# Embedding norm applied on turned rows, with three projection blocks pulled ahead

## The chip, the cores and the metric

The kernel runs on one core of one Trainium2 chip. The metric is device time of one execution in microseconds (us). The core has five engines that each run their own instruction list in order: PE (matrix products and transposes), DVE, ACT and POOL (element-wise work) and SP, which here only issues transfers. Transfers (DMAs) run beside them on queues.

## The reference

The program is two blocks in a row on 1024 tokens of 1024 channels. The first block, cut to what matters:

```python
x = layer_norm(x, ln_emb_g, ln_emb_b)            # (x - mean) * rsqrt(var + eps) * g + b
z = x @ w_in                                     # 1024 x 1984
xs, gs, cq, ckv, kr, gm = split(z)               # 512, 512, 256, 128, 64, 512 channels
ys = s5_branch(xs, ...) * silu(gs)               # state-space model, 32 groups of 16 channels
ym = mla_branch(cq, ckv, kr, ...) * silu(gm)     # latent attention, 4 heads
u  = ALPHA * x + concat(ys, ym) @ w_out
x  = layer_norm(u + sigmoid(u @ w_pg) * (p @ w_pp), ln_g, ln_b)
```

So the normalised x is needed twice: turned (channels on partitions) for `w_in`, and as rows much later, in `u`. The second block (dilated attention, a gated recurrence, a mixture of experts) is not touched.

## The kernel before

**Products.** Everything is fp32, and PE multiplies a shorter type (fp32r). Each operand is therefore split in a high and a low part, and each product is three matmuls: high·high (L178), low·high (L179), high·low (L180). A split takes an ACT copy (the high part, L146 or L150) and a DVE subtraction (the low part, L147 or L153).

**Weights.** `Chunks` loads a weight in chunks of 256 columns (SP, `wraw`, L167), two buffers, and splits each on ACT (`wh`) and DVE (`wl`). `ch.next()` hands out a chunk and issues the loads and splits of the one after it.

**First stage** (`block1`). The eight row tiles x0 to x7 (128 tokens each) are loaded, and the norm's weight and offset are loaded as `lng` and `lnb`, broadcast over 128 partitions (512 KB each). By pairs of tiles, `ln_stats` takes mean and reciprocal deviation on DVE (L443 to L450, and a Newton root, L192 to L205); ACT standardises (L313), POOL multiplies by `lng` (L314), DVE adds `lnb` (L315). The result goes to DRAM as `d_xln` for the much later `u`, and `transpose8` turns it on PE (L215) and splits it into `xTh`, `xTl`.

**Projection and s5.** The `w_in` projection is 32 blocks of 24 matmuls of 128x512 into PSUM (`psG`), 768 in all. The first eight (the `xs` channels, `g_xs`) go through DRAM (`d_xu`) to the s5 branch. `weave` merges three streams by declared costs: `s5_prep` and `s5_groups`; the projection; and rotary tables with small norms. `s5_prep` is a long chain of DVE work on tables (exponentials, sines, `er`, `ei`, `KB`, `KS`), of which line L266 is the first after the exponential's prologue. `s5_groups` runs eight groups; each builds `X1p` (L948), turns it on PE (L965), multiplies (L973, L993), has DVE and its scan make Z and A (L995 to L1004), and multiplies again (L1009 to L1011). The projection's matmuls stand between L993 and L1009 of a group and so fill PE there.

The framework puts each engine's instructions in a fixed order before the run; on the chip an engine waits at the head of its list.

**out_ple** (from L673). The s5 output comes back as `ysf` tiles and is split; the eight row tiles `u` (512 KB each) are loaded from `d_xln`. For each of four blocks of 256 columns and each of eight row tiles, PE makes a block of 24 matmuls of 128x256, and DVE adds it onto `u` (L705). `psG` has few buffers, so PE can go on only as DVE takes the finished blocks.

Of the kernel before, what the change touches and what calls it, by code (L numbers as in the profile page):

```python
# [271 lines left out]
def block1(c):  # L272

    tc, nc, I = c.tc, c.nc, c.I
    d = c.dram
    d_xln = c.d_xln = d.tile([S, D], FT, name="d_xln")
    d_c = c.d_c = d.tile([512, S], FT, name="d_c")
    d_gs = c.d_gs = d.tile([512, S], FT, name="d_gs")
    d_gm = c.d_gm = d.tile([512, S], FT, name="d_gm")
# [11 lines left out]
    xTh = [xp.tile([128, 4, S], FR, name=f"xTh{q}") for q in range(2)]  # L291
    xTl = [xp.tile([128, 4, S], FR, name=f"xTl{q}") for q in range(2)]
    xT = lambda k, sl: (xTh[k // 4][:, k % 4, sl], xTl[k // 4][:, k % 4, sl])
    W = I["w_in"]
    ch = Chunks(c, [(s, 8, True) for s in (
        [W[:, 0:256]], [W[:, 256:512]], [W[:, 1024:1280]], [W[:, 1280:1408], W[:, 1408:1472], W[:, 1408:1472]],
        [W[:, 512:768]], [W[:, 768:1024]], [W[:, 1472:1728]], [W[:, 1728:1984]])]
        + [([I["w_glu"][:, h:h + 256]], 4, False) for h in (0, 256)])

    with ExitStack() as es:  # L300
        pp = c.pool(es, "p0")
        X = [pp.tile([128, D], FT, name=f"x{m}") for m in range(NT)]
        for m in range(NT):
            nc.sync.dma_start(X[m], I["x"][m * 128:(m + 1) * 128, :])
        g_b = pp.tile([128, D], FT, name="lng")
        b_b = pp.tile([128, D], FT, name="lnb")
        nc.scalar.dma_start(g_b, bcast_rows(I["ln_emb_g"], D))
        nc.scalar.dma_start(b_b, bcast_rows(I["ln_emb_b"], D))
        for m0 in range(0, NT, 2):
            for m, (_, mb, r) in zip((m0, m0 + 1), ln_stats(c, X[m0:m0 + 2])):  # L310
                ms = slice(m * 128, (m + 1) * 128)
                x = X[m]
                nc.scalar.activation(x, x, AF.Identity, bias=mb, scale=r)  # L313
                nc.gpsimd.tensor_tensor(x, x, g_b, op=OP.mult)  # L314
                nc.vector.tensor_add(x, x, b_b)  # L315
                nc.sync.dma_start(d_xln[ms, :], x)
                c.dbg("xln", x, lambda o: o[ms, :])
                c.transpose8(x, True, lambda q: (xTh[q][:, :, ms], xTl[q][:, :, ms]))
            if m0 == 2:
                ch.ahead(1)  # L320


    d_xu = c.d_xu = d.tile([8, 128, 4, 128], FT, name="d_xu")
    stage = c.pool(es1, "st", 2)
    half = [slice(0, 512), slice(512, 1024)]
    cols = lambda wk, mb: (wk[0][:, mb * 128:(mb + 1) * 128], wk[1][:, mb * 128:(mb + 1) * 128])
# [4 lines left out]
        nc.scalar.activation(th[:, :n], ps, AF.Tanh, scale=0.5)  # L331
        nc.vector.scalar_tensor_tensor(dst, th[:, :n], 1.0, ps, op0=OP.add, op1=OP.mult)

    def g_xs(n):
        w = ch.next()
        for mb in range(2):
            o = stage.tile([128, 8, 128], FT, name="xo")
            for i, h in enumerate(half):
                ps = c.ps()
                c.gemm(ps, [(cols(w[k], mb), xT(k, h)) for k in range(8)])  # L340
                c.evac(o[:, :, 64 * i:64 * i + 64], ps.rearrange("p (n t) -> p t n", t=8))
                yield 5.2
            for g in range(8):
                b, gg = divmod(16 * n + 8 * mb + g, 4)
                nc.scalar.dma_start(d_xu[b, :, gg, :].rearrange("(t c) n -> c t n", t=8), o[16 * g:16 * g + 16])


    lv = c.con.tile([128, 3, NT], FT, name="lv")
# [7 lines left out]
    def g_latents(js):  # L356
        w = ch.next()
        late = None
        for i, h in enumerate(half):
            for mb, j in enumerate(js):  # L360
                ps = c.ps()
                c.gemm(ps, [(cols(w[k], mb), xT(k, h)) for k in range(8)])
                o = stage.tile([128, 512], FT, name="co")
                nc.vector.tensor_copy(o, ps)
                if late:
                    squares(*late)
                    late = None
# [42 lines left out]
    def rest(cost):  # L410
        yield cost

    gate = lambda o, ps: silu2(o, ps, 512)

    weave((seq(s5_prep(c, es1), s5_groups(c, es1)), 160.0),
          (seq(g_xs(0), g_xs(1), g_latents((0, 1)), g_latents((2, 3)),
               g_feat(d_gs, 0, gate), g_feat(d_gs, 256, gate), g_feat(d_gm, 0, gate), g_feat(d_gm, 256, gate)), 166.4),
          (seq(rest(120.0), rotary_tables(), latent_norms()), 180.0))
    wg = ch.next(), ch.next()
    es1.close()  # L420
# [2 lines left out]
    yp = c.pool(esy, "ym")  # L423
# [6 lines left out]
def seq(*gens):  # L430
    for g in gens:
        yield from g


def ln_stats(c, X):

    nc = c.nc
    n = len(X)
    mv = c.sm([128, n, 2], name="bmv")
    for i, x in enumerate(X):  # L440
        st = c.sm([128, 2, 6], name="bst")
# [231 lines left out]
def out_ple(c, ym, esy):  # L673
    tc, nc, I = c.tc, c.nc, c.I
# [3 lines left out]
    es = ExitStack()  # L678
# [5 lines left out]
    u = [up.tile([128, D], FT, name=f"u{m}") for m in range(NT)]  # L684
    uT = []
    yp = c.pool(esy, "ys")
    ys = [(yp.tile([128, S], FR, name=f"ysh{j}"), yp.tile([128, S], FR, name=f"ysl{j}")) for j in range(4)]
    ns = [slice(n * 256, n * 256 + 256) for n in range(4)]
    ch = Chunks(c, [([I["w_out"][:, s]], 8, False) for s in ns] + [([I["w_pg"][:, s]], 8, True) for s in ns])
    ch.ahead(1)  # L690
    for j in range(4):
        for hs in (slice(0, 512), slice(512, 1024)):
            f = yp.tile([128, 512], FT, name="ysf", bufs=3)
            nc.sync.dma_start(f, c.d_ys[j * 128:(j + 1) * 128, hs])
            c.split(ys[j][0][:, hs], ys[j][1][:, hs], f, scale=0.25)
    for m in range(NT):
# [1 line left out]
    mix = lambda k, m: tuple(a[:, m * 128:m * 128 + 128] for a in (ys + ym)[k])  # L698
    order = (4, 5, 6, 7, 0, 1, 2, 3)
    for n in range(4):  # L700
        w = ch.next()
        for m in range(NT):
            ps = c.ps((128, 256))
            c.gemm(ps, [(mix(k, m), w[k]) for k in order])
            nc.vector.scalar_tensor_tensor(u[m][:, ns[n]], u[m][:, ns[n]], ALPHA, ps, op0=OP.mult, op1=OP.add)  # L705
            if n == 3:
                if m % 2 == 0:
                    uT.append(alloc_aT())
                js = slice((m % 2) * 128, (m % 2) * 128 + 128)
# [50 lines left out]
    g_b = q.tile([128, D], FT, name="plg")  # L760
    b_b = q.tile([128, D], FT, name="plb")
# [4 lines left out]
    w = ch.next(), ch.next()  # L766
    for m in range(NT):
# [4 lines left out]
        x = u[m]  # L772
        ms = slice(m * 128, (m + 1) * 128)
# [25 lines left out]
def s5_prep(c, es):  # L799

    nc, I = c.nc, c.I
# [12 lines left out]
    with ExitStack() as es2:  # L814
        p = c.pool(es2, "s5p")
# [7 lines left out]
        ps = c.psum_tile("T", [128, 2, GR])  # L823
# [47 lines left out]
        nc.vector.tensor_scalar(t["sei"], t["ei"], sg, None, op0=OP.mult)  # L871
        yield 10.0

        q = [p.tile([128, GR], FT, name=f"q{i}") for i in range(5)]
        nc.vector.tensor_mul(q[0], ar, ar)
        nc.vector.tensor_mul(q[1], ai, ai)
        nc.vector.tensor_add(q[0], q[0], q[1])
# [159 lines left out]
class Chunks:  # L1037
# [9 lines left out]
    def next(self):  # L1047
        self.n += 1
        self.ahead(self.n + 1)
        w, self.w[self.n - 1] = self.w[self.n - 1], None  # L1050
        return w
# [957 lines left out]
```

## Time and profile before

| | |
|---|---|
| three runs | 2082.92, 2084.36, 2086.16 us; median 2084.36 |
| the profiled execution | 2080.49 us, of which 2078.7 lie between first and last instruction |
| PE, DVE, ACT, POOL busy | 92%, 72%, 49%, 15% of the span |
| mean granted TensorE clock | 0.958 |
| stages by PE's list | first stage and front of the projection to 195.6, s5 groups to 312.3, `out_ple` from about 495 |

How to read it: PE's share is a mean. Almost all of PE's idle time that bears on the change lies in the first 70 us, where PE waits for the norm, and in short waits up to 520 us. An idle stretch of another engine costs nothing unless PE waits for it later.

### The profile page before, as it was taken

To read this page: it belongs to the slowest core of one execution; us is meant where nothing else is said; L and a number is where in the kernel's file an instruction comes from. 1 tells how busy PE (TensorE), PEld (TensorE's weight loads), DVE (VectorE), ACT (ScalarE), POOL (GpSimd) and SP (SyncE) were. 2 spreads that over 40 slices of the span, in tenths; PEclk is the share of its full clock that TensorE was granted. 3 is DMA by queue.
4 is the path that set the end of the run, shared out by engine and by line. 5 is a ranking of instruction groups with operands and counts; after the bars stand their busy time and mean duration, and the time that the engine had idled before them with its cause. 6 is when DMAs were issued, how large, how long until landed. Compare 5 with 4: busy or idle time off the path is not lost.

```text
span 2078.7 us, 34559 instructions
## 1 busy us (share of the span) xinstructions
PE 1922.5 (92%) x13242; PEld 1705.7 (82%) x13242; DVE 1487.3 (72%) x2909; ACT 1023.7 (49%) x1572; POOL 316.5 (15%) x241
## 2 busy tenths in 40 slices
PE   2999998999999979999999999997899999999992
PEld 2777886888999978898999888897788888888881
DVE  7387677775244967656564556578999999999995
ACT  3223334453132334534432223145788888888883
POOL 3013520000000000000010000013322222222211
PEclk9899999999999989999999998899899999999996
DMA  4344536113131121111111113177899999999974
GB/s 175 100 121 135 157 104 203 41 42 125 44 112 41 59 90 48 57 56 50 48 37 32 42 37 105 61 257 254 302 374 375 379 372 374 358 366 370 355 291 171
DMA packets 143510, 349.14 MB, mean 168 GB/s; under 512 B 33792, under 2 KB 87680, under 8 KB 118768
## 3 DMA queue, kind: packets, MB, share of 16 engines
q1 hardware_dynamic: 127296, 323.81, 43.4%
q0 software_dynamic: 11152, 19.97, 4.0%
q10 hardware_dynamic: 4896, 3.15, 0.7%
q8 instruction: 105, 1.72, 0.3%
q14 instruction: 61, 0.50, 0.1%
HBM read 304.24 MB, written 54.01 MB: 172 GB/s over the span
## 4 chain that ended last, share of the span: by engine, by line
PE 48%; issue 25%; DVE 14%; POOL 5%; DMA 3%; ACT 3%; SPq 0%; POOLq 0%; DVEq 0%; ACTq 0%
PE psG L178 11%; PE psG L179 10%; PE psG L180 10%; POOL gates L1865 3%; PE psT L1303 2%; PE psPO L1254 2%; PE psPO L1387 2%; POOL xg L1865 1%; PE psPO L638 1%; DVE wl L147 1%; PE psSC L1233 1%; DMA wraw<-w_in 1%; PE psSC L1234 1%; PE psT L215 1%; DVE bst L443 1%
## 5 line engine op out<-in xcount | busy, mean ns | idle before, releaser
L1900 DVE TENSOR_TENSOR el<-raw,eh 128x1024 fp32r<-128x1024 f32 x384 | 446.1, 1219 | 31.6 <-ACT eh L1899 31.0
L1899 ACT ACTIVATE eh<-raw 128x1024 fp32r<-128x1024 f32 x384 | 396.8, 1060 | 62.1 <-PE psY L180 25.4
L178 PE MATMUL psG<-aTh,wh 128*128 128x256 f32 x640 | 187.1, 292 | 0.0
L179 PE MATMUL psG<-aTl,wh 128*128 128x256 f32 x640 | 183.6, 287 | 0.0
L180 PE MATMUL psG<-aTh,wl 128*128 128x256 f32 x640 | 183.6, 287 | 0.0
L146 ACT ACTIVATE wh<-wraw 128x512 fp32r<-128x512 f32 (+1 forms) x148 | 91.2, 624 | 181.3 <-PE psG L180 79.1
L147 DVE TENSOR_TENSOR wl<-wraw,wh 128x512 fp32r<-128x512 f32 (+1 forms) x148 | 104.9, 716 | 65.4 <-ACT wh L146 53.5
L178 PE MATMUL psG<-wh,aTh 128*128 128x256 f32 x512 | 146.0, 285 | 0.0
L179 PE MATMUL psG<-wl,aTh 128*128 128x256 f32 x512 | 144.7, 283 | 0.0
L180 PE MATMUL psG<-wh,aTl 128*128 128x256 f32 x512 | 144.1, 281 | 0.0
L178 PEld LDWEIGHTS psG<-aTh,wh 128*128 128x128 f32 x640 | 124.4, 194 | 4.8 <-issue 3.9
L180 PEld LDWEIGHTS psG<-aTh,wl 128*128 128x128 f32 x640 | 124.2, 194 | 1.9 <-issue 1.4
L179 PEld LDWEIGHTS psG<-aTl,wh 128*128 128x128 f32 x640 | 124.4, 194 | 1.4 <-issue 0.9
L180 PE MATMUL psG<-xTh,wl 128*128 128x512 f32 x256 | 103.9, 406 | 4.4 <-DVE wl L147 4.4
L178 PE MATMUL psG<-xTh,wh 128*128 128x512 f32 x256 | 103.7, 406 | 2.1 <-ACT wh L146 1.8
L178 PE MATMUL psY<-eh,hh 128*128 128x512 f32 x256 | 103.0, 402 | 1.7 <-ACT hh L150 1.7
L179 PE MATMUL psG<-xTl,wh 128*128 128x512 f32 x256 | 103.3, 403 | 0.1
L178 PE MATMUL psUU<-eh,xh 128*128 128x512 f32 x256 | 102.8, 402 | 0.0
L178 PE MATMUL psGG<-eh,xh 128*128 128x512 f32 x256 | 101.2, 395 | 0.7 <-ACT xh L146 0.7
L180 PE MATMUL psGG<-eh,xl 128*128 128x512 f32 x256 | 100.9, 394 | 0.0
L180 PE MATMUL psY<-eh,hl 128*128 128x512 f32 x256 | 100.6, 393 | 0.0
L179 PE MATMUL psGG<-el,xh 128*128 128x512 f32 x256 | 100.5, 393 | 0.0
(538 smaller groups left out, 5282.2 us busy)
## 6 DMA issues: line engine op xcount, KB each, us to landing
raw<-w_gate SPq DMA_DIRECT2D x64, 1024.0 KB, 21.6
raw<-w_down SPq DMA_DIRECT2D x64, 1024.0 KB, 22.3
raw<-w_up SPq DMA_DIRECT2D x63, 1024.0 KB, 21.4
wraw<-w_in SPq DMA_DIRECT2D x52, 256.0 KB, 3.0
wraw<-w_in SPq DMA_DIRECT2D x68, 128.0 KB, 2.5
wraw<-w_out SPq DMA_DIRECT2D x32, 256.0 KB, 2.6
x<-x SPq DMA_DIRECT2D x8, 512.0 KB, 8.1
d_xln<-x SPq DMA_DIRECT2D x8, 512.0 KB, 2.6
```

The costliest lines, as they stand in the source:

```text
L146: nc.scalar.activation(h, src, AF.Copy)
L147: nc.vector.tensor_sub(l, src, f32(h))
L178: mm(ps, ah, bh, start=first, stop=False)
L179: mm(ps, ah, bl, start=False, stop=False)
L180: mm(ps, al, bh, start=False, stop=last)
L215: self.nc.tensor.transpose(ps[:, i, :], src, self.ident)
L1254: nc.tensor.matmul(po[64 * j:64 * j + 64], v[:, k, (b % 2) * 128 + 64 * j:(b % 2) * 128 + 64 * j + 64], et[j][:, i, :], start=k == 0, stop ...
L1303: nc.tensor.transpose(ps[:, i, :], e[:, (k0 + i) * 128:(k0 + i + 1) * 128], c.ident)
L1387: nc.tensor.matmul(po[a, cc * 32:cc * 32 + 32], st[a], qi[a, cc * 32:cc * 32 + 32], start=False, stop=cc == cs[-1], skip_group_check=True)
L1865: c.nc.gpsimd.indirect_dma_start(out=dst, out_offset=None, in_=src, in_offset=bass.IndirectOffsetOnAxis(ap=idx, axis=0), bounds_check=src. ...
L1899: nc.scalar.activation(h, src, AF.Copy)
L1900: nc.vector.tensor_sub(l, src, f32(h))
```

## The change

The norm's weight and offset are no longer applied to rows. `standard` only standardises, and `d_xln` holds these plain rows. `turn(h)` turns 512 tokens at a time: per block j of 128 channels four transposes fill one PSUM bank, ACT makes the high part g·x+b as it evicts (L359), and DVE makes the low part in two steps, g·x minus the high part (L361) and plus b (L362). There the weights stand along partitions, so g and b are one number per partition; `lngb` holds them, loaded as 2 x 1024 single elements on ACT's queue. `g_xs` now takes two weight chunks at once and yields by blocks: channel blocks 0 to 2 of the first 512 tokens are issued ahead of the second `turn`. Block 2's halves go out as separate transfers (40 `d_xu` transfers instead of 32). `out_ple` applies weight and offset to `u`: two broadcast loads of 128 KB (`eg`, `eb`) and 16 DVE operations of 128x256 per column block. `ysf` has two buffers instead of three, and s5's table `q` three tiles of its own and two borrowed ones.

```diff
-        g_b = pp.tile([128, D], FT, name="lng")
-        b_b = pp.tile([128, D], FT, name="lnb")
-        nc.scalar.dma_start(g_b, bcast_rows(I["ln_emb_g"], D))
-        nc.scalar.dma_start(b_b, bcast_rows(I["ln_emb_b"], D))
-        for m0 in range(0, NT, 2):
-            for m, (_, mb, r) in zip((m0, m0 + 1), ln_stats(c, X[m0:m0 + 2])):
-                ms = slice(m * 128, (m + 1) * 128)
-                x = X[m]
-                nc.scalar.activation(x, x, AF.Identity, bias=mb, scale=r)
-                nc.gpsimd.tensor_tensor(x, x, g_b, op=OP.mult)
-                nc.vector.tensor_add(x, x, b_b)
-                nc.sync.dma_start(d_xln[ms, :], x)
-                c.transpose8(x, True, lambda q: (xTh[q][:, :, ms], xTl[q][:, :, ms]))
-            if m0 == 2:
-                ch.ahead(1)
+        gb = pp.tile([128, 2, 8], FT, name="lngb")
+        nc.scalar.dma_start(gb[:, 0], I["ln_emb_g"].rearrange("(j p) -> p j", p=128))
+        nc.scalar.dma_start(gb[:, 1], I["ln_emb_b"].rearrange("(j p) -> p j", p=128))
+        def standard(ms):
+            for m, (_, mb, r) in zip(ms, ln_stats(c, [X[m] for m in ms])):
+                nc.scalar.activation(X[m], X[m], AF.Identity, bias=mb, scale=r)
+                nc.sync.dma_start(d_xln[m * 128:(m + 1) * 128, :], X[m])
+        def turn(h):
+            hs = slice(h * 512, h * 512 + 512)
+            for j in range(8):
+                ps = c.psum_tile("T", [128, 512])
+                for m in range(4):
+                    nc.tensor.transpose(ps[:, m * 128:m * 128 + 128], X[4 * h + m][:, j * 128:j * 128 + 128], c.ident)
+                th, tl = xT(j, hs)
+                g, b = gb[:, 0, j:j + 1], gb[:, 1, j:j + 1]
+                nc.scalar.activation(th, ps, AF.Identity, bias=b, scale=g)
+                lo = pp.tile([128, 512], FT, name="lo", bufs=3)
+                nc.vector.scalar_tensor_tensor(lo, ps, g, f32(th), op0=OP.mult, op1=OP.subtract)
+                nc.vector.tensor_scalar(tl, lo, b, None, op0=OP.add)
+        standard((0, 1))
+        standard((2, 3))
+        ch.ahead(1)
+        turn(0)
+        standard((4, 5, 6, 7))
+        xs = g_xs()
+        for _ in range(3):
+            next(xs)
+        turn(1)
...
+    def g_xs():
+        w = ch.next(), ch.next()
+        o = {}
+        for q, i in ((0, 0), (1, 0), (2, 0), (0, 1), (1, 1), (2, 1), (3, 0), (3, 1)):
+            ps = c.ps()
+            c.gemm(ps, [(cols(w[q // 2][k], q % 2), xT(k, half[i])) for k in range(8)])
...
     weave((seq(s5_prep(c, es1), s5_groups(c, es1)), 160.0),
-          (seq(g_xs(0), g_xs(1), g_latents((0, 1)), g_latents((2, 3)),
-               g_feat(d_gs, 0, gate), g_feat(d_gs, 256, gate), g_feat(d_gm, 0, gate), g_feat(d_gm, 256, gate)), 166.4),
+          (seq(xs, g_latents((0, 1)), g_latents((2, 3)),
+               g_feat(d_gs, 0, gate), g_feat(d_gs, 256, gate), g_feat(d_gm, 0, gate), g_feat(d_gm, 256, gate)), 150.8),
...
-            f = yp.tile([128, 512], FT, name="ysf", bufs=3)
+            f = yp.tile([128, 512], FT, name="ysf", bufs=2)
...
     for n in range(4):
+        g_n, b_n = (yp.tile([128, 256], FT, name=f"e{q}") for q in "gb")
+        nc.sync.dma_start(g_n, bcast_rows(I["ln_emb_g"][ns[n]], 256))
+        nc.sync.dma_start(b_n, bcast_rows(I["ln_emb_b"][ns[n]], 256))
         w = ch.next()
         for m in range(NT):
             ps = c.ps((128, 256))
             c.gemm(ps, [(mix(k, m), w[k]) for k in order])
+            nc.vector.tensor_tensor(u[m][:, ns[n]], u[m][:, ns[n]], g_n, op=OP.mult)
+            nc.vector.tensor_tensor(u[m][:, ns[n]], u[m][:, ns[n]], b_n, op=OP.add)
             nc.vector.scalar_tensor_tensor(u[m][:, ns[n]], u[m][:, ns[n]], ALPHA, ps, op0=OP.mult, op1=OP.add)
```

DVE's list at the start of s5's long chain (L266), before: six projection blocks have been copied out by then, the last two of them as `xo`.

```order
L261 TENSOR_SCALAR exr<-exr 128x32
L141 COPY xo<-psG 128x8x64 x2
L147 TENSOR_TENSOR wl<-wraw,wh 128x512 x2
L266 TENSOR_SCALAR exk<-exr 128x32
L267 RECIPROCAL exk<-exk 128x32
L268 SCALAR_TENSOR_TENSOR exr<-exr,exk 128x32
```

The same place after (L391 is the copy of a latent block's `psG`):

```order
L261 TENSOR_SCALAR exr<-exr 128x32
L147 TENSOR_TENSOR wl<-wraw,wh 128x512 x2
L141 COPY co<-psG 128x512
L141 COPY xo<-psG 128x8x64
L391 COPY co<-psG 128x512 x3
L266 TENSOR_SCALAR exk<-exr 128x32
L267 RECIPROCAL exk<-exk 128x32
```

L266 moved behind the copies of eleven blocks (264 matmuls) from behind six (144). On PE the first group's transposes (L965, now L998) moved from behind 480 projection matmuls to behind 534.

PE's list at the last group of s5, after (L998, L1006, L1026 and L1042 to L1044 are the former L965, L973, L993 and L1009 to L1011):

```order
L1042 MATMUL psT<-Mt_1487,U 128x128
L1043 MATMUL psT<-Q_2356,A_1489 128x128
L1044 MATMUL psT<-Q_2357,A_1490 128x128
L998 MATMUL psT<-ident,X1p 128x128 x4
L1006 MATMUL psT<-Q_2515,KB 16x128 x4
L1026 MATMUL psT<-U,BT_2533 128x128 x4
L1026 MATMUL psT<-U,BT_2534 128x128 x4
L1042 MATMUL psT<-Mt_1488,U 128x128
```

Before, 29 projection matmuls stood between the L993 and the L1009 of this group, and 36 in the group ahead of it; now there are none and 12. The earlier groups have 36 to 39.

SP's list at the start of `out_ple`, before (u_4605 is the first row tile of eight):

```order
L694 DMA ysf<-d_ys 128x512 x3
L697 DMA u_4605<-d_xln 128x1024
L694 DMA ysf<-d_ys 128x512 x3
L697 DMA u_4606<-d_xln 128x1024
L694 DMA ysf<-d_ys 128x512 x2
L697 DMA u_4607<-d_xln 128x1024
```

Here `u` follows three `ysf` loads at a time, and nothing stands behind the last `u`. The end of the same piece after:

```order
L724 DMA u_4606<-d_xln 128x1024
L724 DMA u_4607<-d_xln 128x1024
L721 DMA ysf<-d_ys 128x512 x2
L724 DMA u_4608<-d_xln 128x1024
L724 DMA u_4609<-d_xln 128x1024
L730 DMA eg<-ln_emb_g 128x256
L731 DMA eb<-ln_emb_b 128x256
```

The row tiles are now u_4602 to u_4609. The `ysf` loads go by twos with two `u` loads behind each pair, and the first `eg` and `eb` stand behind all of them.

## Rows read from the trace of the kernel before

**Rows 1.** Stretches by time: busy us (instructions) of each engine, PE's granted clock, DMA share, GB/s

```profile
0.00:63.00 63.00, 21.25 (x88) 16.52 (x88) 51.12 (x108) 22.20 (x30) 21.38 (x12) 0.92 0.45 173
50.00:60.00 10.00, 8.22 (x34) 6.56 (x34) 9.70 (x10) 5.34 (x9) 4.91 (x2) 0.67 0.57 210
103.50:195.60 92.10, 84.58 (x376) 69.95 (x374) 77.73 (x190) 28.85 (x46) 19.16 (x19) 0.93 0.42 125
195.60:312.30 116.70, 116.34 (x705) 100.54 (x706) 79.17 (x140) 38.79 (x77) 45.60 (x34) 0.98 0.48 133
510.00:520.00 10.00, 7.52 (x60) 7.31 (x61) 3.37 (x8) 1.26 (x2) 0.00 (x0) 1.00 0.93 334
```

**Rows 2.** Groups by line and shape, 0 to 70 us: busy us, mean ns, idle before

```profile
L314 POOL TENSOR_TENSOR x<-x,lng 128x1024 f32<-128x1024 f32 x8 | 21.2, 2665 | 35.0 <-ACT x L313 35.0
L315 DVE TENSOR_TENSOR x<-x,lnb 128x1024 f32<-128x1024 f32 x8 | 16.9, 2145 | 2.3 <-POOL x L314 2.3
L215 PE MATMUL psT<-ident,x 128*128 128x128 f32 x64 | 13.2, 378 | 38.1 <-DVE x L315 35.0 <-DVE xTl L147 3.1
```

**Rows 3.** Timeline of DVE, first stage: start, duration, instruction, idle before

```profile
19.33 2.33 DVE L205 SCALAR_TENSOR_TENSOR rs_o<-rs_b,rs_o 128x2 f32<-128x2 f32 x1
...
21.66 2.31 DVE L195 TENSOR_SCALAR rs_h<-bve 128x2 f32<-128x2 f32 x1
...
25.57 0.14 DVE L450 SCALAR_TENSOR_TENSOR bmb<-bmv,brs 128x2 f32<-128x2 f32 x1
...
60.43 1.22 DVE L315 TENSOR_TENSOR x<-x,lnb 128x1024 f32<-128x1024 f32 x1
```

**Rows 4.** Timeline of PE, to 200 us

```profile
27.38 1.97 PE L215 MATMUL psT<-ident,x 128*128 128x128 f32 x8 [27.38 <-DVE x L315]
...
53.75 0.63 PE L179 MATMUL psG<-xTl,wh 128*128 128x512 f32 x1
54.17 0.63 PE L180 MATMUL psG<-xTh,wl 128*128 128x512 f32 x1
...
63.16 0.99 PE L178 MATMUL psG<-xTh,wh 128*128 128x512 f32 x2 [0.24 <-ACT xTh L146]
...
165.16 0.39 PE L180 MATMUL psG<-xTh,wl 128*128 128x512 f32 x1
165.38 0.39 PE L178 MATMUL psG<-xTh,wh 128*128 128x512 f32 x1
...
195.63 1.09 PE L965 MATMUL psT<-ident,X1p 128*128 128x128 f32 x4 [4.65 <-DVE X1p L948]
```

**Rows 5.** Timeline of DVE, 98 to 215 us

```profile
101.64 0.69 DVE L141 COPY xo<-psG 128x512 f32<-128x512 f32 x1 [12.91 <-PE psG L180]
103.45 0.17 DVE L266 TENSOR_SCALAR exk<-exr 128x32 f32<-128x32 f32 x1
...
123.24 0.43 DVE L232 TENSOR_SCALAR sdk<-sdk 128x512 f32<-128x512 f32 x1
```

**Rows 6.** What DVE waited for, 103.4 to 195.5 us: us in total, times, longest

```profile
DVE co L364 <- PE psG L180: 4.8, 2, 2.7
DVE xo L141 <- PE psG L180: 2.4, 1, 2.4
```

**Rows 7.** Timeline of DVE in the last s5 group

```profile
302.78 0.67 DVE L995 TENSOR_TENSOR Z<-psT,cos 128x512 f32<-128x512 f32 x1
...
308.11 0.74 DVE L1004 SCALAR_TENSOR_TENSOR A<-Z,cst,sin 128x508 f32<-128x508 f32 x1
```

**Rows 8.** Timeline of DVE at the start of `out_ple`

```profile
518.11 0.42 DVE L705 SCALAR_TENSOR_TENSOR u<-u,psG 128x256 f32<-128x256 f32 x1 [0.87 <-DMA u<-d_xln]
```

**Rows 9.** Timeline of PE at the start of `out_ple`

```profile
514.18 0.39 PE L178 MATMUL psG<-wh,ymh 128*128 128x256 f32 x1 [0.94 <-DVE u L705]
```

**Rows 10.** DMA issues by line: count, KB each, median us from issue to landing

```profile
ysf<-d_ys SPq DMA_DIRECT2D x8, 256.0 KB, 3.4
gq<-q_norm_g SPq DMA_DIRECT2D x1, 1.0 KB, 8.9
lb<-hgrn_gamma SPq DMA_DIRECT2D x1, 4.0 KB, 3.0
```

More of the change, by code (lines that the diff above doesn't have):

```diff
@@ L294, in block1 @@
     W = I["w_in"]
-    ch = Chunks(c, [(s, 8, True) for s in (
+    ch = Chunks(c, [(s, 8, False) for s in (
         [W[:, 0:256]], [W[:, 256:512]], [W[:, 1024:1280]], [W[:, 1280:1408], W[:, 1408:1472], W[:, 1408:1472]],
@@ L298, in block1 @@
         + [([I["w_glu"][:, h:h + 256]], 4, False) for h in (0, 256)])
[L300 to L304, printed above, removed]
-        g_b = pp.tile([128, D], FT, name="lng")
-        b_b = pp.tile([128, D], FT, name="lnb")
-        nc.scalar.dma_start(g_b, bcast_rows(I["ln_emb_g"], D))
-        nc.scalar.dma_start(b_b, bcast_rows(I["ln_emb_b"], D))
-        for m0 in range(0, NT, 2):
-            for m, (_, mb, r) in zip((m0, m0 + 1), ln_stats(c, X[m0:m0 + 2])):
-                ms = slice(m * 128, (m + 1) * 128)
-                x = X[m]
-                nc.scalar.activation(x, x, AF.Identity, bias=mb, scale=r)
-                nc.gpsimd.tensor_tensor(x, x, g_b, op=OP.mult)
-                nc.vector.tensor_add(x, x, b_b)
-                nc.sync.dma_start(d_xln[ms, :], x)
-                c.dbg("xln", x, lambda o: o[ms, :])
-                c.transpose8(x, True, lambda q: (xTh[q][:, :, ms], xTl[q][:, :, ms]))
-            if m0 == 2:
-                ch.ahead(1)
     d_xu = c.d_xu = d.tile([8, 128, 4, 128], FT, name="d_xu")
@@ L332, in silu2 @@
         nc.vector.scalar_tensor_tensor(dst, th[:, :n], 1.0, ps, op0=OP.add, op1=OP.mult)
[L334 to L345, printed above, removed]
+    def g_xs():
[4 more added lines that the diff above has]
+            c.gemm(ps, [(cols(w[q // 2][k], q % 2), xT(k, half[i])) for k in range(8)])
+            n0, n1 = 64 * i, 64 * i + 64
+            if q == 2:
+                d = stage.tile([128, 512], FT, name="co").rearrange("p (t n) -> p t n", t=8)
+                full, first, last = d, n0, True
+            else:
+                if i == 0:
+                    o[q] = stage.tile([128, 8, 128], FT, name="xo")
+                full, first, last = o[q], 0, i == 1
+                d = full[:, :, n0:n1]
+            c.evac(d, ps.rearrange("p (n t) -> p t n", t=8))
+            yield 5.2
+            for g in range(8 if last else 0):
+                b, gg = divmod(8 * q + g, 4)
+                nc.scalar.dma_start(d_xu[b, :, gg, first:n1].rearrange("(t c) n -> c t n", t=8), full[16 * g:16 * g + 16])
@@ new lines, in block1 @@
+    with ExitStack() as es:
+        pp = c.pool(es, "p0")
+        X = [pp.tile([128, D], FT, name=f"x{m}") for m in range(NT)]
+        for m in range(NT):
+            nc.sync.dma_start(X[m], I["x"][m * 128:(m + 1) * 128, :])
+        gb = pp.tile([128, 2, 8], FT, name="lngb")
[26 more added lines that the diff above has]
+        turn(1)
@@ L872, in s5_prep @@
         yield 10.0
-        q = [p.tile([128, GR], FT, name=f"q{i}") for i in range(5)]
+        q = [p.tile([128, GR], FT, name=f"q{i}") for i in range(3)] + [dt, dr]
         nc.vector.tensor_mul(q[0], ar, ar)
```

## The prediction

> **What bounds the kernel now.** I read the stretches by time first [rows 1]. In the first 63 us PE is busy 21.3; from 195.6 to 312.3 it is busy 116.3 of 116.7. So the first stage is bound by what feeds PE, and the s5 groups by PE. The groups by line name the feeder: PE's transposes wait 35.0 us for DVE's `lnb` addition (L315), which waits for POOL's multiplication at 2.67 us each [rows 2]. PE's timeline gives two marks: transposes begin at 27.38, and steady matmuls at 63.16, when 26 of the 768 projection matmuls are done [rows 4]. Between 103.5 and 195.6 PE is busy 84.6 of 92.1 and DVE 77.7 [rows 1]; there the question is which comes last. PE then waits 4.65 us at 195.63 for `X1p` [rows 4], so DVE's s5 chain ends last; but DVE itself stood 7.2 us for PE's blocks [rows 6], so the two held each other up. At the start of `out_ple` transfers take 0.93 of the queues and PE is busy 7.5 of 10 [rows 1].
>
> **First stage.** Eight POOL operations (21.2 us) and eight DVE additions (16.9) go [rows 2]. They also held other work. Two operations on 128x2 take 2.33 and 2.31 us at 19.33 and 21.66, while POOL multiplies from 19.3; a like one takes 0.14 at 25.57 [rows 3]. The L315 addition takes 1.22 once POOL has ended [rows 3], 2.15 in the mean [rows 2]. The Trainium skill (SBUF — State Buffer, "SBUF: two separate sides") says that GpSimd and VectorE share a port pair under an exclusive lock and the loser blocks. These rows agree; with POOL out of this stage the inflation should vanish altogether.
>
> So the statistics of x2, x3, ready at 25.6, come at 25.6 − 4.3 ≈ 21.3, and two normalisations put x3 at about 24. PE can begin turning then instead of alternating with L315. DVE now needs per channel block L361 (128x512) and L362. A 128x512 `TENSOR_SCALAR` took 0.43 [rows 5]; the old subtraction starts every 0.60. No row has L362's rounded output. Below, the plain 0.43, started every 0.34; above, 0.60 like the subtraction. I take the first, since it is the nearest instruction. Then one `turn` is 8 × 0.94 = 7.5 us of DVE (9.6 above), plus weight splits in between, and ends near 35 (37 to 39). Three blocks of 24 matmuls at 0.227 [rows 4] are 16.3 us; they follow the tiles closely and end near 46. The second `turn` ends near 54, with 105 matmuls issued. Against 26 at 63.16 PE is 9 us early and 79 × 0.227 = 18 us of work further: a lead of 27 us.
>
> **What becomes of the lead.** This decides the forecast. s5's chain cannot start early, because L266 now stands on DVE behind eleven blocks (264 matmuls) rather than six (144). Before, 144 were done at 101.6 [rows 5]: from 63.16, 118 matmuls took 38.5 us, of which 118 × 0.227 = 26.8 and the other 11.7 small transposes and slow-clock matmuls. After: 159 × 0.227 = 36, plus about 10, from 54 makes 100. L266 gains only about 3 us on its 103.45 [rows 5].
>
> From L266 to `X1p` took 92.1 us, 77.7 of it DVE's own work [rows 1]. The 7.2 us of waits for PE [rows 6] go, as PE is ahead, and about 1 us of block copies lies ahead of L266 now. The waits for POOL and ACT stay. So 92.1 − 8.2 ≈ 84, and `X1p` is ready at 184 instead of 195.5. PE has to give back most of its lead waiting for weight splits (`wl`) that stand among the same DVE operations. Bounds: 7 us less if the chain follows at DVE's pure busy time (177), 6 more if waits for PE stay (190). Gain at the first group: 11 us (5 to 18).
>
> At that point 534 projection matmuls stand ahead in PE's order, not 480: 54 × 0.227 = 12.3 us less is left. But they were cover. In the last group 6.1 us passed on DVE between the first Z and the end of A [rows 7], with a copy and a weight split of 0.6 each in it; alone some 4.6. The last group now has no matmuls to hide that, the one ahead 12 × 0.227 = 2.7 us: 4.6 + 1.9 ≈ 6 us of waiting returns (4 to 9). Front gain: 11 + 12.3 − 6 ≈ 17 us (10 to 25).
>
> Two edits I cost at nothing: s5's shared `q` tiles, and eight more `d_xu` issues on ACT, which is busy 28.9 of 92 us [rows 1]. Without that cover, and each as long as a 128x512 subtraction (0.6 from start to start), they would be 5 us.
>
> **out_ple.** Sixty-four DVE operations of 128x256 are added, each near the 0.42 of the existing one [rows 8]: 27 us, beside PE's matmuls, DVE being a third busy [rows 1]. Hidden, except at the start. The first block's `u` needs `eg` and `eb`, and these stand last in SP's list, behind all eight `u` loads. Before, the second `psG` round began at 514.18, one `u` tile being enough [rows 9], and the fifth landed at about 518 [rows 8], with the queues at 0.93 and 334 GB/s [rows 1]. Two `ysf` buffers also make SP issue by pairs: load (3.4 us [rows 10]), split, next pair, three times over. So `eg` lands about 520 (517.5 to 521), and three operations later, near 522, PE has a free `psG`: 8 us lost (4 to 11). Nothing else on PE's list can fill it. Later columns' pairs have 23 us each, and cost nothing. This time counts as if nothing were shifted; the front gain moves all of it alike.
>
> **Sum.** From the profiled 2080.5: −11 − 12.3 + 6 + 8 ≈ −9.3, or 2071.2. That execution was 3.9 below the median, so about 2075 in the median runs.
>
> **Rivals.**
> A. PE keeps its lead. If DVE's chain is not what ends last, the whole 27 us pass on, less 8 in `out_ple`: 2065. For it: DVE is idle 14 us between 103 and 195. Against: PE already waits for `X1p`, and the chain's start moves by 3 only. A hidden `eg` wait (transfers landing with the `u` tiles) leads to 2067 in the same way. Together 0.18.
> B. Gain too small to tell: `X1p` at 190 and both losses at their upper ends, −5.6 − 12.3 + 9 + 11 ≈ +2, to −3: 2081 to 2088. Chance 0.18.
> C. Slower, by PE's clock. The first stage's matmuls now alternate with transposes and waits for two evicting engines. In the 50 to 60 stretch, with just such alternation, the granted clock was 0.67 [rows 1] and matmuls stood 0.43 apart instead of 0.227 [rows 4], which is PE at the lower of its two levels. If all 105 run so, 105 × 0.2 = 21 us are lost before the second `turn` ends, and L266, behind the 264th matmul, starts at 121, not 100. Then `X1p` comes at 205: 2075 + 21 ≈ 2096. In general the gain is 110 minus L266's start, so it turns at 110, and beyond 114 is seen as slower. For it: that row. Against: PE has 16 us of matmuls in one stretch without waits. Chance 0.09.
> D. `lngb` lands late. Its loads are of single elements. An element-wise load of 1024 elements (`lb`) took 3.0 us, one of 256 (`gq`) 8.9 [rows 10]; by the latter's pace 36 us. ACT needs it at 24; landing at 38, it would cost 14 us, at 2089. The Trainium skill (DMA: Bandwidth & Descriptors, "Rules for kernel authors") warns that a non-contiguous last dimension becomes one descriptor per element. The row for `lb` bears out the form but not a high price. Chance 0.05.
>
> **How the numbers follow.** Forecast (2068 to 2081) 0.50, A 0.18, B 0.18, C 0.09, D 0.05. A change under 0.2% (4.2 us) can't be told from none here: faster is below 2080.2, slower above 2088.5. Faster takes A and most of the forecast, 0.65; slower C, half of D and a part of B, 0.14; the same 0.21. The range 2062 to 2088 leaves out C's centre and the ends; the forecast's own is 2068 to 2081.
>
> **What would show it.** Right: the first L356 transposes near 19 to 25; the second `turn` over by 57; L266 near 100; a wait of 10 us of PE for `wl` near 110; first L998 near 185; waits of 2 and 4.6 us ahead of L1042 in the last two groups; 8 us of PE waiting for `u` in `out_ple`. Wrong: L266 after 110, small operations on DVE still taking over 2 us, `eg` landing before the last `u` tile, or no wait for `wl` (then A).

## The result and the profile after

The changed kernel took 2097.87 us, the median of 5 runs (2094.76 to 2102.8), against 2084.36 for the kernel before: a ratio of 1.0067 [1.0054, 1.0079], so 13.5 us slower where 2075 was forecast. The profiled execution's span is 2095.9 us (2078.7 before), 17.2 more; the profiled execution of the kernel before lay 3.9 below its median, so 13.5 is the measure of the whole, and the two traces serve to say where it arises. Three marks on DVE, read in both traces, say where: the last attention copy `yo` starts 5.0 us later than before (505.04 against 500.07), `out_ple`'s first `u` with the projection 14.6 later (528.28, L738, against 513.72), and the first `wpr` load 17.15 later (620.27 against 603.12). After that nothing moves. So the front, where −17 was forecast, gave +5, and `out_ple`, where +8 was forecast, gave about +12.

Stretches of the changed kernel (from:to, length, then busy us and instructions of PE, weight load, DVE, ACT, POOL; PE's granted clock, DMA share, GB/s). The first two are those of [rows 1]; the last runs from the first turned `X1p` to the end of s5:

```profile
0.00:63.00 63.00, 44.16 (x205) 35.03 (x206) 43.88 (x128) 29.70 (x39) 0.20 (x4) 1.00 0.58 200
103.50:195.60 92.10, 71.75 (x312) 58.98 (x311) 76.48 (x178) 32.16 (x50) 19.28 (x19) 0.86 0.41 125
110.00:130.00 20.00, 11.56 (x45) 9.80 (x45) 16.04 (x56) 5.13 (x8) 3.51 (x3) 0.54 0.16 46
194.41:313.90 119.49, 109.31 (x652) 95.25 (x653) 78.74 (x139) 37.35 (x75) 43.74 (x34) 0.92 0.50 134
```

and of the kernel before, the last two again:

```profile
110.00:130.00 20.00, 20.00 (x89) 16.54 (x89) 13.43 (x46) 4.73 (x7) 3.52 (x3) 1.00 0.40 99
195.63:312.44 116.81, 116.48 (x706) 100.65 (x707) 79.17 (x140) 38.79 (x77) 45.57 (x34) 0.98 0.49 133
```

The first stage did what it was to do: PE is busy 44.2 of 63 us instead of 21.3, at clock 1.00 instead of 0.92, and at 63.16 its trace has 140 projection matmuls begun where the one before has 24: 116 × 0.227 ≈ 26 us of work, the lead that was forecast. But from 103.5 to 195.6 PE is busy 71.8 instead of 84.6. In 110 to 130, where PE was busy all 20 us before at clock 1.00, it is busy 11.6, and its granted clock is 0.54: the lower level, 1.2 GHz, nearly throughout. From the first `X1p` to the end of s5 the work is 54 matmuls smaller (652 records against 706), as forecast, but it takes 119.5 us instead of 116.8: PE stands idle for 10.2 of them (0.3 before), and its granted clock is 0.92 (0.98). So the 5.0 at `yo` in these two executions are made up of −1.2 at the first `X1p`, +2.7 in the s5 groups and +3.5 from there to `yo`.

What PE waited for up to 630 us, largest first (who waited, whom for: us in total, times, longest), of the changed kernel:

```profile
PE psT L356 <- ACT x L347: 18.2, 2, 17.2
PE psT L1042 <- DMA Mt<-R: 10.2, 2, 6.1
PE psT L998 <- DVE X1p L981: 8.5, 1, 8.5
PE psG L178 <- ACT ysh L150: 6.6, 3, 3.0
PE psG L180 <- DVE wl L147: 6.3, 1, 6.3
PE psT L380 <- ACT th L397: 5.5, 2, 3.4
PE psG L179 <- DVE yl L153: 4.3, 3, 3.1
...
PE psG L178 <- DVE u L738: 3.6, 1, 3.6
```

The first row is the start of the kernel. The wait for `X1p` grew from 4.65 [rows 4] to 8.5. The waits for `th` stood nowhere in the forecast. Those ahead of L1042 did, but smaller and by another path than `Mt`, and `ysh` stood there only as a reason for `eg` to come late.

**First stage.** DVE's timeline answers to [rows 3] (start, duration, instruction, idle before):

```profile
17.21 0.14 DVE L205 SCALAR_TENSOR_TENSOR rs_o<-rs_b,rs_o 128x2 f32<-128x2 f32 x1
...
23.27 1.40 DVE L361 SCALAR_TENSOR_TENSOR lo<-psT,lngb,xTh 128x512 f32<-128x512 f32 x2
24.59 0.87 DVE L362 TENSOR_SCALAR xTl<-lo,lngb 128x512 fp32r<-128x512 f32 x2
25.38 1.40 DVE L361 SCALAR_TENSOR_TENSOR lo<-psT,lngb,xTh 128x512 f32<-128x512 f32 x2
```

The 128x2 operation takes 0.14 us where it took 2.33 beside POOL. Two channel blocks take 2.11 us of DVE (23.27 to 25.38), so one takes 1.05 where 0.94 was said and 1.20 was the upper bound. PE's timeline answers to [rows 4]:

```profile
17.21 2.25 PE L356 MATMUL psT<-ident,x 128*128 128x128 f32 x8 [17.21 <-ACT x L347]
...
121.70 0.79 PE L180 MATMUL psG<-xTh,wl 128*128 128x512 f32 x1 [6.32 <-DVE wl L147]
...
194.41 1.09 PE L998 MATMUL psT<-ident,X1p 128*128 128x128 f32 x4 [8.53 <-DVE X1p L981]
```

Transposes begin at 17.21 instead of 27.38. Yet the first `X1p` is turned at 194.41 instead of 195.63: of the ten us that the transposes are early, one is left 177 us later. In between DVE's timeline answers to [rows 5]:

```profile
100.99 0.69 DVE L391 COPY co<-psG 128x512 f32<-128x512 f32 x1 [4.75 <-PE psG L180]
101.60 0.17 DVE L266 TENSOR_SCALAR exk<-exr 128x32 f32<-128x32 f32 x1
```

s5's chain (L266) starts 1.85 us earlier than before, behind the eleventh block's copy: DVE had stood 4.75 us for that block, with all its other work done. From there to the turned `X1p` it took 92.8 us (92.2 before), of which DVE's own work is 77.7, as before. What DVE waited for in those 92.8, beside [rows 6] (4.7 of the first row's 7.2 lie just ahead of L266, so 2.5 belong here):

```profile
DVE co L391 <- PE psG L180: 7.2, 3, 4.7
DVE dg L973 <- DMA dg<-d_skip: 3.0, 1, 3.0
DVE ang L431 <- DMA d_xu<-xo: 2.3, 1, 2.3
DVE sdk L230 <- POOL al L947: 1.9, 1, 1.9
DVE lv L381 <- PE psT L380: 1.8, 1, 1.8
```

**The last groups.** SP's issues and PE's waits there (`Mt` is a table that eight small transfers fill from `R` for each group):

```profile
302.81 5.06 SPq L1012 DMA_DIRECT2D Mt<-R x8
```

```profile
294.51 0.77 PE L1042 MATMUL psT<-Mt,U 128*128 128x128 f32 x2 [4.03 <-DMA Mt<-R]
309.23 0.77 PE L1042 MATMUL psT<-Mt,U 128*128 128x128 f32 x2 [6.14 <-DMA Mt<-R]
...
322.86 0.80 PE L179 MATMUL psG<-yl,wh 128*128 128x512 f32 x1 [3.14 <-DVE yl L153]
```

`R` is ready on DVE at 302.78 (L1009). Eight DMAs to `Mt` follow, issued one after the other at 0.6 us each, the last landing 1.8 us later, just before 309.23. DVE's path through Z to A, which the forecast priced, ends at 308.5 and is not the last, though it alone would by this trace have held PE up to there. Before, both lay under projection matmuls. The last two groups together, after and before:

```profile
284.17:313.90 29.73, 19.55 (x120) 17.68 (x119) 16.72 (x31) 7.86 (x17) 4.17 (x4) 0.77 0.50 138
285.32:312.44 27.12, 27.12 (x173) 23.61 (x172) 17.05 (x32) 9.41 (x19) 4.17 (x4) 1.00 0.33 86
```

With 53 matmuls fewer they took 2.6 us longer: PE was idle for 10.2 us, and its granted clock was 0.77 instead of 1.00.

**out_ple.** DVE's timeline beside [rows 8], and SP's issues ahead of it:

```profile
526.93 0.76 DVE L736 TENSOR_TENSOR u<-u,eg 128x256 f32<-128x256 f32 x2 [2.43 <-DMA eg<-ln_emb_g]
...
528.28 0.74 DVE L738 SCALAR_TENSOR_TENSOR u<-u,psG 128x256 f32<-128x256 f32 x2
```

```profile
507.75 0.92 SPq L721 DMA_DIRECT2D ysf<-d_ys x2
...
512.96 1.81 SPq L721 DMA_DIRECT2D ysf<-d_ys x2
...
517.66 2.37 SPq L721 DMA_DIRECT2D ysf<-d_ys x2
520.07 0.91 SPq L724 DMA_DIRECT2D u<-d_xln x2
521.01 0.43 SPq L730 DMA_DIRECT2D eg<-ln_emb_g x1
```

`ysf` goes out in pairs 5 us apart, and `eg` behind everything, as forecast. PE waited three times for a pair (`ysh`, 6.6 us) and then 3.6 for `u`; before, 2.0 and 0.9. That is 7.3 us more. The stretch from `yo` to `wpr` before and after, and a piece of it after:

```profile
500.07:603.12 103.05, 99.97 (x823) 98.62 (x822) 37.44 (x69) 21.59 (x37) 0.00 (x0) 1.00 0.26 85
505.04:620.27 115.23, 104.95 (x823) 103.02 (x822) 58.88 (x133) 21.69 (x37) 0.00 (x0) 0.93 0.26 88
520.00:535.00 15.00, 9.19 (x42) 8.89 (x43) 8.55 (x23) 1.26 (x2) 0.00 (x0) 0.51 0.35 122
```

The same 823 matmuls leave PE idle for 10.3 us instead of 3.1, and they keep it busy for 105.0 instead of 100.0. During and behind those waits PE's granted clock was 0.51, the lower level, from 520 to 535; before, it was 1.00 throughout. So of the 12.2 us some 7.2 are waiting and 5.0 are slower matmuls.

### The profile page after: what moved, and what is told of

Same layout as the page of the kernel before. It is cut to its first block, busy times and chain, and to the rows that moved or that the text cites. A ratio compares the mean times of both kernels' runs of the same rounds, so it can differ in the third digit from the quotient of the medians.

```text
span 2095.9 us, 34644 instructions
## 1 busy us (share of the span) xinstructions
PE 1929.8 (92%) x13242; PEld 1712.9 (82%) x13242; DVE 1495.1 (71%) x2967; ACT 1028.4 (49%) x1574; POOL 292.3 (14%) x233
## 3 DMA queue, kind: packets, MB, share of 16 engines
q10 hardware_dynamic: 7840, 2.11, 0.6%
## 4 chain that ended last, share of the span: by engine, by line
PE 37%; issue 24%; DVE 11%; POOL 5%; DMA 4%; ACT 2%; SPq 0%; POOLq 0%; DVEq 0%; ACTq 0%
PE psG L178 8%; PE psG L179 7%; PE psG L180 7%; POOL gates L1898 3%; PE psT L1336 2%; PE psPO L1287 2%; PE psPO L1420 1%; POOL xg L1898 1%; PE psPO L665 1%; PE psSC L1266 1%; PE psSC L1267 1%; DMA wraw<-w_in 1%; DVE Sc L1406 1%; DVE wl L147 1%; PE psSC L1398 1%
## 5 line engine op out<-in xcount | busy, mean ns | idle before, releaser
L180 PE MATMUL psUU<-eh,xl 128*128 128x512 f32 x256 | 100.3, 392 | 0.0
L179 PE MATMUL psY<-el,hh 128*128 128x512 f32 x256 | 100.0, 391 | 0.3 <-DVE el L1933 0.3
```

The costliest lines, as they stand in the source:

```text
L179: mm(ps, ah, bl, start=False, stop=False)
L180: mm(ps, al, bh, start=False, stop=last)
```

## The experiments

Ratios are against the kernel before on the same chip, with 95% intervals. The theory at the start, from the trace above: the front's lead is lost because s5's chain stands behind eleven blocks and its last groups are bare (Rival T below: the bare groups are all of it), and `out_ple` costs some 12 us by itself.

**The front alone.** Out of the change: `ysf` back to three buffers, and the loads and operations of `eg` and `eb` left out, so `u` lacks weight and offset.

```diff
-            f = yp.tile([128, 512], FT, name="ysf", bufs=2)
+            f = yp.tile([128, 512], FT, name="ysf", bufs=3)
-            nc.vector.tensor_tensor(u[m][:, ns[n]], u[m][:, ns[n]], g_n, op=OP.mult)
-            nc.vector.tensor_tensor(u[m][:, ns[n]], u[m][:, ns[n]], b_n, op=OP.add)
```

> The change without its part in out_ple: the norm's weight and offset are left out of u altogether, no eg and eb loads, ysf back to three buffers; the first stage and all up to out_ple as changed. Theory (the front brings nothing, out_ple costs about 12): the traces put the changed kernel 5.0 us behind at the start of out_ple and 17.2 behind after it, with the profiled run of before 3.9 under its median, so this kernel should come within 2084 to 2090, and out_ple's first u operation should stand where before's stood plus 5. Rival 1 (the front alone loses it all, through the uncovered s5 groups and a late glu): 2095 or more. Rival 2 (the front does gain its 17 and out_ple costs 30): 2070 or less.

Measured: 2084.42, 0.9999 [0.9984, 1.0013]. Its trace has the same waits (`Mt` 10.1, `X1p` 8.4, `wl` 6.3, `th` 6.3). The front gains nothing. In its trace `yo` stands at 504.79, 4.7 later than before; but that execution lies 3.8 above its median and the profiled one of the kernel before 3.9 below, so the +5 is no more than executions of one kernel differ by.

**`out_ple` alone.** The kernel before with only the change's edits there (the weights and offsets are then applied twice).

> The kernel before with only out_ple changed: eg and eb loads, 64 added DVE operations, two ysf buffers (so weight and offset are applied a second time to u). Theory: the loads by pairs and eg behind all u cost 10 to 12 us: 2094 to 2097. Rival (the loss in out_ple comes from what the front hands over, not from its own loads): 2083 to 2087. My blind figure was 8: 2092.

Measured: 2096.1, 1.0048 [1.0029, 1.0067], about +10 by the ratio, and 11.4 at the marks of its trace. PE waits 8.8 us for `ysh` and 2.0 for `u`. The two halves add up to the change: 0 and 10 to 12, of 13.5.

**No blocks ahead of the second turn.** `xs` runs wholly behind `turn(1)`, at the old share of 166.4.

```diff
-        for _ in range(3):
-            next(xs)
         turn(1)
...
-               ...), 150.8),
+               ...), 166.4),
```

> The change without the three blocks ahead of the second turn: all xs blocks after it, and the projection's share of the merge back at 166.4. On DVE the copies of one block instead of seven then stand ahead of L266, and the s5 groups have 36 to 43 and at the end 29 matmuls, as before. Theory D (the lead is lost because s5's long DVE chain starts behind eleven blocks and the last groups are bare): L266 comes before 90 instead of 101.6, the first X1p turn at 178 to 184 instead of 194, no wait for Mt in the last groups, and the time is 12 to 18 us under the changed kernel's, 2080 to 2086, out_ple's loss still in it. Rival P (the chain's length, not its start, sets the first group, as it took 92.0 us in both kernels while its waits changed): X1p within 4 us of 194 and the time within 2093 to 2099.

Measured: 2071.56, 0.9941 [0.9925, 0.9957], better than any theory gave. DVE's timeline (two rows) and PE's:

```profile
51.83 0.18 DVE L266 TENSOR_SCALAR exk<-exr 128x32 f32<-128x32 f32 x1 [0.30 <-ACT exr L262]
...
89.69 0.69 DVE L389 COPY co<-psG 128x512 f32<-128x512 f32 x1 [15.14 <-PE psG L180]
```

```profile
173.79 1.09 PE L996 MATMUL psT<-ident,X1p 128*128 128x128 f32 x4 [4.82 <-DVE X1p L979]
```

Without the three blocks L266 stands at 51.83 instead of 101.60, and `X1p` is turned at 173.79, with 480 matmuls ahead as in the kernel before. No group waits for `Mt`; `wl` is waited for 1.7 us. Without the blocks ahead and at the old share the kernel is 26 us faster: the blocks had taken their matmuls to a place where PE was idle, but drawn the start of the longest chain behind eleven blocks. This run changes both, the start and the share that covers the last groups; the run with the share alone, below, takes them apart. L266 came 50 us earlier and `X1p` only 21, since DVE then stood for PE's blocks in the chain, once for 15.14 us (up to 89.69).

**s5's first steps ahead of the weave.** The change, but five steps of s5's preparation are written ahead of the weave, and its share is lowered by as much.

```diff
-    weave((seq(s5_prep(c, es1), s5_groups(c, es1)), 160.0),
+    s5 = s5_prep(c, es1)
+    for _ in range(5):
+        next(s5)
+    weave((seq(s5, s5_groups(c, es1)), 126.0),
```

> The change, with s5_prep run up to its exponentials ahead of the merge (its share then 126 of 160): L266 stands behind the copies of two blocks on DVE, X1p's turn behind 428 matmuls instead of 534, and the last groups have 41 and 31 matmuls. Theory D: L266 near 70 to 80, X1p at 165 to 175, the front 20 us ahead of the changed kernel's: 2074 to 2080. Rival P: X1p moves by less than half of what L266 moves, since DVE then works beside the first blocks' splits and copies, and the time is 2088 or more.

Measured: 2076.83, 0.9956 [0.9941, 0.9971]; L266 at 60.84, `X1p` turned at 161.96 with 428 matmuls ahead, no `Mt` wait. With the blocks kept ahead, 21 us come back, so the blocks as such did not cost the time. But here too two things changed: the chain starts 41 us earlier, and the lower share leaves 106 more matmuls behind the first `X1p`, which cover the groups again.

**Only the share.** 150.8 becomes 115: s5's first group stands behind 480 projection matmuls again instead of 534.

> The change with nothing but the projection's share of the merge set from 150.8 to 115. L266 stays behind the same seven copies on DVE, but X1p's turn stands behind 480 matmuls instead of 534, and the last two s5 groups have 36 and 33 matmuls instead of 12 and none. Theory D (the start of s5's chain sets the front; a matmul ahead of the first group is worth as much as one under a later group): X1p's turn again at 192 to 196, no wait for Mt, the glu begins 2 to 5 us earlier than in the changed kernel: 2092 to 2096. Rival T (the bare last groups, which cost 10.2 us of waiting for Mt plus slow matmuls behind it, are the loss, and the 54 matmuls ahead were free since PE idles there): 10 to 14 us under the changed kernel's, 2083 to 2088.

Measured: 2086.04, 1.0005 [0.9994, 1.0016], 11.8 below the change, as Rival T had it; the theory that only the chain's start counts missed. PE's timeline, and the stretch from L266 to the turned `X1p` in the change and here:

```profile
181.69 1.09 PE L998 MATMUL psT<-ident,X1p 128*128 128x128 f32 x4 [10.30 <-DVE X1p L981]
```

```profile
101.60:194.40 92.80, 72.45 (x316) 59.72 (x315) 77.72 (x189) 32.09 (x49) 18.16 (x19) 0.87 0.41 124
```

```profile
102.39:181.70 79.31, 59.70 (x255) 48.91 (x253) 72.79 (x169) 22.32 (x38) 25.60 (x19) 0.84 0.41 121
```

The first of the two is the change, the second this run. L266 stands where it stood; the chain is 13.5 us shorter. Of that 4.9 is DVE's busy time, 4.1 of it six evictions of `co` (L310, 0.68 each) that stand inside the change's stretch and behind it here. The other 8.6 is idle time (15.1 against 6.5): the waits for `dg`, `al`, `lv` and for PE's blocks in the list above are gone. That the evictions are the reason for these waits too was not shown. With the chain done 12.7 us earlier and 54 matmuls back among the groups, no group waits for `Mt`. So about 12 of the 26 us come back by the share alone, with the chain's start where it was; the other 14.5 (2086.04 less 2071.56, both with 480 matmuls ahead of `X1p`) are what leaving out the blocks, and with it the earlier start, adds (9.2 with the five steps ahead).

**`eg` and `eb` loaded ahead of `ysf`.** From here on all start from the version without blocks ahead (2071.56).

```diff
+    e0 = eload(0)
...
+        g_n, b_n = e0 if n == 0 else eload(n)
```

(`eload` holds the change's three lines.)

> e3_no_ahead (2071.6) with the first eg and eb loads issued ahead of the ysf loads instead of behind all u loads; two ysf buffers stay. Theory E (the wait for eg, 3.6 us in e3's trace, and the three operations behind it cost about 6 of the 12 us): 2064 to 2067. Rival Y (the two ysf buffers set the pace, with 7.6 us of PE waiting for ysh, and eg only lands beside them): 2069 to 2073.

Measured: 2067.94, 0.9909 [0.9891, 0.9927]: 3.6 less, between the two ranges expected. The wait for `u` is gone, the `ysh` waits stay (6.4).

**Two buffers, nothing else.** No `eg`, no `eb`, none of the 64 operations (`u` lacks weight and offset), `ysf` with two buffers.

> e3_no_ahead with two ysf buffers but without eg, eb and the 64 added operations (u lacks the norm's weight and offset). Here the scheduler puts the ysf loads ahead of most u loads. With three buffers and no eg this front should give about 2060 (2071.6 less the 11.5 that the part in out_ple cost in the other two kernels). Theory E: two buffers alone cost 2 to 4 us: 2062 to 2064. Rival Y: they cost most of it: 2067 to 2071.

Measured: 2057.76, 0.9867 [0.9851, 0.9884], below every range expected. Two `ysf` buffers alone are not the cause of the pairs: here five loads go out first, and DVE's first split (L153) starts at 474.49, ahead of the last attention copy at 478.18:

```profile
474.49 1.29 DVE L153 SCALAR_TENSOR_TENSOR ysl<-ysf,ysh 128x512 fp32r<-128x512 f32 x2
478.18 0.69 DVE L684 SCALAR_TENSOR_TENSOR yo<-psPO,gm 128x512 f32<-128x512 f32 x1 [1.67 <-PE psPO L663]
```

**`u` loads on POOL's queue.** As the run with `eg` first, but `nc.gpsimd.dma_start(u[m], ...)`.

> e6_eg_first with the eight u loads issued by POOL, which is idle there, so that SP's list holds the ysf loads alone and none waits behind a u load in its queue. Theory E: ysf lands in its 2.6 to 3.4 us and PE's waits for ysh shrink from 7.6 to about 4: 2061 to 2065. Rival: the loads share the same 334 GB/s whatever queue issues them, and all eight u loads now start ahead of the later ysf loads, so PE waits longer for ysh: 2070 or more.

Measured: 2073.36, 0.9944 [0.9926, 0.9962], 5.4 worse than on SP. The `ysh` waits grew to 9.3, as the rival had it: all eight `u` loads (4 MB) went out between 478.9 and 483.2, where SP's order had spread them among the pairs of `ysf` from 480.5 to 494.5, and one `ysf` load took 8.3 us to land (at most 4.7 before). That the loads compete is read from these times; a third queue, which would tell it from a peculiarity of POOL's, was not tried.

**`eg` and `eb` in `u`'s pool.** As the run with `eg` first, but in pool `up`, so that `yp` is 2 KB per partition smaller.

```diff
-        e = [yp.tile([128, 256], FT, name=f"e{q}") for q in "gb"]
+        e = [up.tile([128, 256], FT, name=f"e{q}") for q in "gb"]
```

> e6_eg_first (2067.9) with eg and eb kept in the pool of the u tiles instead of the pool of ysh and ysl. That pool is then 2 KB per partition smaller, as in e7_two_bufs, and the scheduler places the first ysf splits ahead of the last attention steps and five ysf loads ahead of u. Theory M (the part in out_ple costs 12 us because the pool, grown into memory that attention still uses, pushes the ysf splits behind attention's end, so that ysf loads by pairs fall among the u loads; and because eg lands last): both causes gone, 2058 to 2061, near e7_two_bufs' 2057.8, and under both kernels. Rival O (the 64 added DVE operations themselves delay PE once the loads are in time): 2064 to 2068.

Measured: 2058.39, 0.9875 [0.9858, 0.9891], the lower end of the expectation. Beside the run in which the 64 operations are left out (2057.76) they cost 0.6, inside the intervals. DVE's order there, and then in the change:

```profile
472.48 1.28 DVE L153 SCALAR_TENSOR_TENSOR ysl<-ysf,ysh 128x512 fp32r<-128x512 f32 x2
476.18 0.69 DVE L684 SCALAR_TENSOR_TENSOR yo<-psPO,gm 128x512 f32<-128x512 f32 x1 [1.67 <-PE psPO L663]
```

```profile
505.04 0.69 DVE L686 SCALAR_TENSOR_TENSOR yo<-psPO,gm 128x512 f32<-128x512 f32 x1 [1.67 <-PE psPO L665]
507.04 1.29 DVE L153 SCALAR_TENSOR_TENSOR ysl<-ysf,ysh 128x512 fp32r<-128x512 f32 x2
```

The splits stand ahead of the last copy again; in the change they stand behind it. Moving two tiles of 1 KB per partition from one pool to the other was enough to move them, for 9.5 us against the run with `eg` first.

**That `out_ple` on the change's own front.**

> The change with e9's out_ple: eg and eb in the pool of u, the first pair loaded ahead of ysf; the front as changed. Theory M: out_ple's cost goes, and what is left is the front alone, as e1_front_only: 2084 to 2088. Rival O: 2090 to 2096.

Measured: 2085.35, 1.0002 [0.9992, 1.0012], 12.5 below the change. So `out_ple`'s 12 us and the front's nothing are separate.

**In `u`'s pool, but loaded last.**

> e3_no_ahead (2071.6) with eg and eb in the pool of u, but still loaded last, behind all u loads. Tells the two causes of theory M apart. If the pool's place is most of the cost: 2058 to 2062. If eg landing behind eight u tiles is most of it (my blind step: PE free again 8 us later): 2065 to 2069.

Measured: 2070.1, 0.9936 [0.9919, 0.9952], 11.7 above the version with `eg` loaded first, and above both ranges expected.

```profile
496.94 0.76 DVE L734 TENSOR_TENSOR u<-u,eg 128x256 f32<-128x256 f32 x2 [5.97 <-DMA eg<-ln_emb_g]
```

PE waits 9.4 us for `u` here. Either fault alone, the pool (9.5) or the late load (11.7), costs nearly what both cost together (13.2, from 2071.56 to 2058.39): they are two paths to the same block, and the longer one counts.

**The best version at a share of 150.**

> e9_eg_in_u_pool with the projection's share 150 instead of 166.4: X1p's turn behind 471 matmuls instead of 480, and 38 instead of 29 matmuls in the last s5 group. If matmuls under the last group are worth more than those ahead of the first, as e5_share115 showed on the change: 1 to 3 us under e9. If the chain's end is all that counts: the same within 1 us.

Measured: 2057.64, 0.9868 [0.9851, 0.9884]: the same as at 166.4, so more matmuls under the last group gained nothing here. The two best versions are 27 us faster than the kernel before and 40 faster than the change.

## Why the prediction was wrong

**First stage: right.** Sum, order and the vanishing of the inflated operations came as worked out, and sooner: transposes at 17.21 (19 to 25 said), PE at full clock to the end of the second `turn`, which DVE ends at 53.4 (54 said). L266 at 101.6 (100 said) and a wait for `wl` at 121.7 (10 us near 110 said; 6.3 came) are right too, though 5.5 us of waits for `th` came just ahead of it. So is the lead of 27 us. `lngb` landed within 5 us of its issue, so D is out.

**"So 92.1 − 8.2 ≈ 84": the first step that failed.** The chain took 92.8 from L266. I took DVE's 7.2 us of waits for PE as going, 1 us of its work as lying ahead, and all else as it was. But 2.5 of those waits stayed (`co`), 1.8 came at `lv`, and transfers were waited for longer: `dg` 3.0 instead of 0.9, and `ang` 2.3. DVE's own work stayed at 77.7. What I had not asked is what the blocks ahead of the first group do to the chain: with 54 matmuls taken out from there the chain took 79.3.

**"54 × 0.227 = 12.3 us less is left": counted as a gain beside the 11.** The runs gave one or the other. With the 54 matmuls left behind the chain, it took 79.3 and `X1p` was turned at 181.69, even before the 184 of the forecast; with them ahead, 92.8. Nor did they shorten what follows: the last two groups, 53 matmuls poorer, took 29.7 us instead of 27.1. In the kernel before they ran while the groups' own steps (`Mt`, Z to A) were under way; taken out, they left that time behind as waits.

**"4.6 + 1.9 ≈ 6 us of waiting returns": right in kind, too small, and the wrong path.** 10.2 came, through `R` and the eight DMAs of `Mt`, not DVE's Z and A. From `R` to the last landing takes 8 × 0.6 + 1.8 ≈ 6.6, and I had not looked at who else releases L1042. A further 3.1 at `yl` followed behind the last group.

Together these turned −17 into +5 in the profiles, and into nothing in the medians. Rival C's time (2096) is close to what was measured, but its mechanism is not what happened: no clock fell in the first stage, and L266 was at 101.6, not 121. The clock fell later: to 0.60 in 70 to 75, with PE busy throughout, and to 0.54 in 110 to 130, where PE waited for `th` and `wl`. The traces can split the loss: up to `yo` both kernels have 2433 matmul records; PE's idle time is 64.4 us before and 66.4 after, its busy time 435.7 and 438.6. So the 22.9 us of idle time that the first stage saved came back later, with 2.1 more and 2.9 of slower matmuls on top.

**"8 us lost (4 to 11)": right as a wait, too small as a cost.** 10 to 12 were lost. PE's idle time grew by 7.2, near the 8, though 6.6 us were waited for `ysh` and only 3.6 for `u`; `eg` landed by 526.9, which is 521.9 without the front's 5.0, where 517.5 to 521 was said. What the step left out is what the waits do to PE behind them: 5.0 us of slower matmuls, at a granted clock of 0.51. I also put the pairs down to two buffers and thought nothing of the pools. Two buffers alone are harmless (2057.76); the pairs need the splits behind the last attention copy as well. That the 64 operations are hidden was right.

What stays open is why the scheduler places the splits ahead of the copy when `eg` and `eb` are not in `yp`: only that it does was seen. In the five runs with 4 KB per partition of `ysf`, `eg` and `eb` in `yp` they stand ahead; with 6 KB (the change, the run with `eg` first, the kernel before and all others) behind.

## What to carry to other kernels

An engine's lead is worth what the next chain can take of it: before adding up, follow where the longest chain of the next stage starts, and put no block in front of that start, even one that fills idle time. Work moved ahead of a wait brings its evictions along; count it as a gain only if the waiting chain's engine doesn't run them, and if the place it leaves did not need it as cover. Price a wait of PE with the matmuls behind it: here 7.2 us of waiting were followed by 5.0 of slower matmuls. Load small operands that a first block needs ahead of the large ones, and look at what a few KB more or less in a pool do to the order of the engines' lists.

## What was not expected of the hardware

With POOL out of the stage, DVE's 128x2 operations fell from 2.33 to 0.14 us; that much had been read off before. New is that moving 4 MB of `u` loads from SP's queue to POOL's made the kernel 5.4 us slower, most likely because the queue had served as an order. And PE's granted clock was 0.54 from 110 to 130, where PE was busy 11.6 of 20 us, and 0.51 from 520 to 535 behind its waits for `ysh` and `u`; in the kernel before, both stretches were fully busy at 1.00.
